# Squares moved by 4 transfers instead of 16, and scaling chains issued ahead of splits, in a hybrid decoder block

## The chip, the cores and the metric

The kernel runs on one core of one Trainium2 chip. The metric is the device time of one execution in microseconds (us). The kernel before was timed in three runs: 2091.04, 2091.20 and 2092.34 us, median 2091.2. The engines are TensorE (PE: matrix products and transposes by a product with the identity), VectorE (DVE), ScalarE (ACT), GpSimd (POOL) and SyncE (SP), which here issues the DMA transfers. Each engine runs its own list of instructions in order and waits on semaphores for the others.

## What is computed

One layer of a pre-norm decoder block for 2048 tokens of width 1024, in float32:

```
h = rmsnorm(x, norm_mix_g);  u = h @ w_in
y_conv = gate_b * conv3(gate_c * v)
y_rnn  = rg_lru(conv4(x_r)) * gelu(g)
y = concat[rmsnorm(y_conv, g_norm_conv), rmsnorm(y_rnn, g_norm_rnn)]
x = x + y @ w_out
h = rmsnorm(x, norm_mlp_g)
x = x + square(relu(h @ w_mlp_in)) @ w_mlp_out
return rmsnorm(x, final_norm_g)
```

Here the seam between `y @ w_out` and `h @ w_mlp_in` matters: x gets its last term from w_out, is squared and summed over each token's row, scaled by 1/rms and by norm_mlp_g, and has to be turned (from tokens on partitions to the 1024 features on partitions) before it can be multiplied by w_mlp_in.

## The kernel before

The 2048 tokens are four blocks of 512 (TB), worked in pairs: blocks 0 and 1, then 2 and 3. A product of float32 matrices is made of three passes of rounded parts (hi and lo: a tile `w_hi` that ACT casts and a tile `w_lo` that DVE subtracts), and large products follow a fast scheme with 7 products in place of 8. In w_out these are numbered 6, 5, 3, 7, 4 at the place in question, each for one half (512 columns) of x in one or both blocks of the pair. `product(i, ...)` goes over the four token tiles t of a block in the order 0, 2, 1, 3 (TORDER, n counts the steps): PE multiplies (`multiply`, line 2103, result `wo_x` in PSUM), DVE adds the result to x (`add`, line 2116), then the function `behind(n, t)` issues whatever is to run beside it: `in_third` behind product 3, `in_seventh` behind 7, `in_fourth` behind 4. Products 3, 7 and 4 share few PSUM buffers, so a step of one waits for an add of the product ahead.

Between w_out and the MLP the two blocks of a pair go different ways, both from a scaled tile `xs` (line 2377 on DVE, 2378 on ACT, one half each; the scale comes from `square`, line 2354 on ACT, and the chain of small instructions in `root`, lines 2365 to 2372).

- The first block (b) is turned without PE. DVE transposes 32x32 squares of `xs` into the tile `cut` (line 2391); then `move_squares` (line 2400) has the DMA queue move them to their partitions, into four tiles `raw0`, 16 transfers of 128 KB: for each of 4 token tiles a, 32 partitions of `cut` to 32 partitions of `raw0[a]`, 4 times. `gain_rows` (line 2421) multiplies by norm_mlp_g, `first_hi` (2425, ACT) and `first_lo` (2430, DVE) split the tiles into operands H.
- The second block (b + 1) is turned by PE: `turn` (line 1984) makes eight transposes of `xs` into PSUM, and ACT copies them out with the gain (line 1991).

The x of the second block's first half comes from DRAM by two loads of 512 KB (`load_x_half`, line 2122). Product 7 adds to its other half, product 4 to this one. Behind product 4 come the up products of the MLP (`ups`, line 662): `ups[s].prepare(i)` splits a weight tile (lines 197 and 198), and `drain` takes results out of PSUM (line 691 on ACT, 695 on DVE, tile `snap`). The first two turns stand between product 4's last steps, the other two between the first up products; the text writes up (s, i) for product i of column block s.

The order on each engine is the order in which the code issues the work, but for pieces wrapped in `tc.high_priority(n)`, which puts them n places ahead, and in `tc.issue_after`. The lists are the same in both pairs; the second pair's place lies 1018.44 us behind the first's.

Of the kernel before, what the change touches and what calls it, by code (L numbers as in the profile page):

```python
# [11 lines left out]
AF = mybir.ActivationFunctionType  # L12
# [3 lines left out]
P = 128  # L16
SEQ = 2048
D = 1024
# [73 lines left out]
def block_kernel(  # L92
# [213 lines left out]
    def x_half(b, t, dh):  # L306
        return xt[b, t // 2, dh][:, t % 2, :]
# [1810 lines left out]
    def load_x_half(b, dh):  # L2118
        for th in range(2):
            r = temp("x")  # L2120
            r0 = b * TB + th * 256
            nc.sync.dma_start(
                r,
                x[r0 : r0 + 256, dh * 512 : dh * 512 + 512].rearrange("(t p) d -> p t d", p=P),
            )
            xt[b, th, dh] = r
# [8 lines left out]
    def pair_before_mlp(b, ups, by_hand):  # L2135
# [10 lines left out]
        def load(n):  # L2146
            for i, g in todo[:n]:
                o.load(i, g)
            del todo[:n]
# [224 lines left out]

        def scaled(b, t, rs):
            xs[t] = temp("xs")
            V.tensor_scalar(xs[t][:, 1, :], x_half(b, t, 1), rs, None, MUL)
            nc.scalar.activation(xs[t][:, 0, :], x_half(b, t, 0), AF.Copy, scale=rs)
            keep_half(b, t)

        def in_fifth(n, t):
# [14 lines left out]
        def move_squares():  # L2396
            raw0.extend(temp("raw0", (P, KD, P)) for _ in range(4))
            for a in range(4):
                for g in range(4):
                    nc.sync.dma_start(  # L2400
                        raw0[a][32 * g : 32 * g + 32],
                        cut[0][32 * a : 32 * a + 32, g].rearrange("p k t i -> p k (t i)"),
                    )

        def in_third(n, t):
            prepare(7, of(1, 0), n)
            square(b, t, 1)
            scaled(b, t, root(b, n, t))
            cut_squares(t)
            if n == 3:  # L2410
                load(3)
                move_squares()

        product(5, Y, True, in_fifth)
        product(3, Y, False, in_third)
        ups[0].load((0,))
        load_x_half(b + 1, 0)
        hw = []

        def gain_rows(a):  # L2420
            tt(raw0[a], raw0[a], gm[:, :, None].broadcast_to([P, KD, P]), MUL)
# [10 lines left out]
        def in_seventh(n, t):  # L2432
            prepare(4, of(1, 1), n)
            square(b + 1, t, 1)
            if n > 1:
                for a in (2 * n - 4, 2 * n - 3):
                    gain_rows(a)
            if n == 3:
                hw.extend(first_operands())
                for a in range(4):  # L2440
                    first_hi(0, a)
                for a in range(4):
                    first_lo(0, a)

        product(7, X, False, in_seventh)
        for a in range(4):
            first_hi(1, a)
        ups[1].load((0,))
        r1 = []

        def in_fourth(n, t):
            square(b + 1, t, 0)
            if n == 0:
                ups[0].prepare(ORDER[0])
            if n < 2:
                first_lo(1, 2 * n)
                first_lo(1, 2 * n + 1)
            if n == 2:
                ups[0].prepare(ORDER[1])
                r1.extend(temp("r1") for _ in range(4))  # L2460
            if n > 1:
                turn(xs[TORDER[n - 2]], TORDER[n - 2], r1, gm)
            scaled(b + 1, t, root(b + 1, n, t))

        product(4, X, False, in_fourth)
        ups[1].prepare(ORDER[0])
# [34 lines left out]
    def mlp(b, ups, r0, r1, t2, rest, fifth, xs, turns_at, prepared):  # L2501
# [6 lines left out]
        for n in range(-LEAD1, len(seq)):  # L2508
            m = n + LEAD1
            if prepared <= m < len(seq):  # L2510
                ups[seq[m][0]].prepare(seq[m][1])
            m = n + SUMS1
            if 0 <= m < len(seq):
                ups[seq[m][0]].sums(seq[m][1])
# [8 lines left out]
            if s == NS - 1 and i in (3, 4):  # L2523
                with tc.issue_after(made_at["snap"]):
                    downs[0].prepare(1, i - 3)
            ups[s].drain(i, Z)
            if n == 0:
                ups[2].load((0,))
            if n in turns_at:
# [162 lines left out]
```

## Time and profile before

| | |
|---|---|
| runs | 2091.04, 2091.20, 2092.34 us |
| the profiled execution | 2091.45 us, span from first to last instruction 2089.7 us, 1.75 us around it |
| PE busy | 2074.5 us, 99% of the span |
| DVE busy | 1633.5 us, 78% |
| ACT busy | 1137.6 us, 54% |
| DMA | 226 GB/s over the span |

A row of the timeline is one instruction or several of a kind (x8), with its start, its length, and in brackets how long the engine idled before it and which instruction or transfer ended that. A transfer's row on SP is only its issue; it lands later.

### The profile page before, as it was taken

What the parts mean: (1) busy time and instruction counts of PE and PEld (TensorE: products, weight loads), DVE (VectorE), ACT (ScalarE), POOL (GpSimd) and SP (SyncE); (2) the same over time, 40 slices, a digit from 0 to 9 for tenths busy, and PEclk for the clock granted to TensorE, in tenths of its full rate; (3) what the DMA queues carried; (4) which work ended last, traced back from release to release, by engine and by line L of the source; (5) the groups of instructions that cost most, each with busy time, mean ns of one, the idle gap of its engine ahead of it and who ended that gap; (6) DMA issues with size and microseconds to landing.
All of it is one profiled execution on the core that took longest, in us unless ns stands there. A gap on an engine that the chain in (4) does not pass through costs nothing.

```text
span 2089.7 us, 24956 instructions
## 1 busy us (share of the span) xinstructions
PE 2074.5 (99%) x9262; PEld 1707.0 (82%) x9262; DVE 1633.5 (78%) x1867; ACT 1137.6 (54%) x1485; POOL 46.4 (2%) x75
## 2 busy tenths in 40 slices
PE   9999999999999999999999999999999999999998
PEld 8888788878888888888888887887788888888887
DVE  6789898579766878999987776876876665887776
ACT  6789863366655544444555887233853333533344
POOL 0011000000000000000000100000000000000000
PEclk9999999999999999999999999999999999999999
DMA  9489688763788687777384557676353445844432
GB/s 341 163 304 326 246 329 343 261 213 117 258 317 283 256 301 303 270 285 279 121 312 168 205 181 271 243 272 221 127 186 114 169 161 211 343 151 151 141 121 81
DMA packets 200330, 477.77 MB, mean 229 GB/s; under 512 B 15504, under 2 KB 80016, under 8 KB 200208
## 3 DMA queue, kind: packets, MB, share of 16 engines
q1 hardware_dynamic: 198608, 471.45, 62.5%
q10 hardware_dynamic: 1568, 4.72, 0.6%
q8 instruction: 73, 1.20, 0.2%
q14 instruction: 49, 0.40, 0.1%
q0 software_dynamic: 32, 0.00, 0.0%
HBM read 313.58 MB, written 158.33 MB: 226 GB/s over the span
## 4 chain that ended last, share of the span: by engine, by line
PE 79%; DVE 8%; ACT 5%; issue 2%; DMA 1%; SPq 0%; POOL 0%; DVEq 0%; ACTq 0%; POOLq 0%
PE up L662 39%; PE dn L785 28%; PE wo_x L2103 4%; PE wo_w L2103 3%; PE wo_y L2103 2%; DVE xr L1303 1%; ACT r L1324 1%; DVE v L1360 1%; PE ps_b L256 1%; ACT gi L1331 1%; DMA x<-in_x_dram 1%; PE psri L1771 1%; ACT r L1991 1%; DVE w_lo L1244 1%; PE ps_c L256 1%
## 5 line engine op out<-in xcount | busy, mean ns | idle before, releaser
L662 PE MATMUL up<-H,w_hi 128*128 128x512 f32 x2576 | 795.2, 390 | 1.9 <-DVE snap L695 1.9
L662 PEld LDWEIGHTS up<-H,w_hi 128*128 128x128 f32 x2576 | 482.1, 188 | 105.3 <-ACT snap L691 2.6
L662 PE MATMUL up<-H,w_lo 128*128 128x512 f32 x1288 | 501.3, 389 | 0.0
L785 PE MATMUL dn<-w_hi,z_hi 128*128 128x512 f32 x864 | 336.1, 389 | 0.0
L785 PE MATMUL dn<-w_lo,z_hi 128*128 128x512 f32 x864 | 336.1, 389 | 0.0
L785 PE MATMUL dn<-w_hi,z_lo 128*128 128x512 f32 x864 | 336.1, 389 | 0.0
L662 PEld LDWEIGHTS up<-H,w_lo 128*128 128x128 f32 x1288 | 241.7, 188 | 50.5 <-DVE w_lo L198 0.2
L197 ACT CAST z_hi<-z 128x1024 fp32r<-128x1024 f32 x112 | 118.0, 1053 | 289.4 <-PE dn L785 243.9
L198 DVE TENSOR_TENSOR w_lo<-w,w_hi 128x1024 fp32r<-128x1024 f32 x156 | 190.0, 1220 | 78.5 <-ACT w_hi L197 29.0
L197 ACT CAST w_hi<-w 128x1024 fp32r<-128x1024 f32 x156 | 163.0, 1049 | 116.3 <-PE up L662 61.5
L785 PEld LDWEIGHTS dn<-w_hi,z_lo 128*128 128x128 f32 x864 | 162.2, 188 | 33.8
L785 PEld LDWEIGHTS dn<-w_hi,z_hi 128*128 128x128 f32 x864 | 162.2, 188 | 33.7
L785 PEld LDWEIGHTS dn<-w_lo,z_hi 128*128 128x128 f32 x864 | 162.2, 188 | 33.5
L817 DVE TENSOR_TENSOR x<-dn,x 128x1024 f32<-128x1024 f32 x108 | 130.9, 1218 | 22.3 <-PE dn L785 22.1
L198 DVE TENSOR_TENSOR z_lo<-z,z_hi 128x1024 fp32r<-128x1024 f32 x112 | 136.2, 1216 | 3.1 <-ACT z_hi L197 3.1
L2103 PE MATMUL wo_x<-w_o,y_hi 128*128 128x512 f32 x384 | 118.9, 391 | 1.6 <-DVE x L2116 1.6
L2103 PEld LDWEIGHTS wo_x<-w_o,y_hi 128*128 128x128 f32 x384 | 71.6, 188 | 17.2 <-DVE x L2116 2.5
L679 ACT ACTIVATE snap<-snap 128x1024 f32<-128x1024 f32 x36 | 38.2, 1061 | 71.5 <-DVE snap L707 27.6
L2103 PE MATMUL wo_x<-w_o,y_lo 128*128 128x512 f32 x192 | 74.9, 390 | 0.0
L2103 PE MATMUL wo_w<-w_o,y_hi 128*128 128x512 f32 x192 | 59.0, 389 | 0.0
L674 ACT COPY snap<-up 128x1024 f32<-128x1024 f32 x32 | 32.4, 1014 | 39.4 <-PE up L662 34.6
L198 DVE TENSOR_TENSOR w_lo<-t,w_hi 128x1024 fp32r<-128x1024 f32 x32 | 39.0, 1218 | 18.8 <-PE dn L785 14.3
(430 smaller groups left out, 3201.9 us busy)
## 6 DMA issues: line engine op xcount, KB each, us to landing
z<-d_z SPq DMA_DIRECT2D x112, 512.0 KB, 5.6
w_o<-d_sum SPq DMA_DIRECT2D x84, 512.0 KB, 7.1
w<-in_w_mlp_in_dram SPq DMA_DIRECT2D x64, 512.0 KB, 6.7
d_z<-snap SPq DMA_DIRECT2D x64, 512.0 KB, 3.1
d_sum<-sum_hi SPq DMA_DIRECT2D x49, 512.0 KB, 4.8
d_z<-z SPq DMA_DIRECT2D x48, 512.0 KB, 3.4
w<-in_w_mlp_out_dram SPq DMA_DIRECT2D x48, 512.0 KB, 8.7
raw<-in_w_in_dram SPq DMA_DIRECT2D x30, 512.0 KB, 6.8
```

The costliest lines, as they stand in the source:

```text
L197: nc.scalar.copy(hi, src)
L198: return (lo_engine or V).tensor_tensor(lo, src, hi.bitcast(F32), SUB).ins
L256: nc.tensor.matmul(ps[:, j, :], ws[k // 4][:, k % 4, j * P : (j + 1) * P], hs(k), start=k == 0 and i == 0, stop=k == KD - 1 and i == len(p ...
L662: nc.tensor.matmul(ps[:, j, :], ws[:, k, j * P : (j + 1) * P], hs(k), start=i in (1, 2, 5) and k == 0 and n == 0, stop=k == 3 and n == len ...
L674: made_at["snap"] = nc.scalar.copy(t, ps).ins
L679: nc.scalar.activation(t, t, AF.Relu)
L785: nc.tensor.matmul(ps[t // 2][:, t % 2, :], zs[:, p, t * P : (t + 1) * P], ws[:, p, :], start=i in (1, 2, 5) and a == 0 and p == 0 and n == 0,
L817: V.tensor_add(xt[b, th, dh], ps[th], xt[b, th, dh])
L1244: tt(lo, r, hi.bitcast(F32), SUB)
L1303: stt(o, x_in[:, j, k : k + TB], par("rnn_conv_w", 8 * k + c), o, MUL, ADD)
L1324: nc.scalar.activation(r[own, j, :], ps[own, e, :], AF.Sigmoid, bias=par("b_a", c)[own])
L2103: nc.tensor.matmul(ps[t // 2][:, t % 2, :], ys[:, j, t * P : (t + 1) * P], ws[:, j, :], start=first and n == 1, stop=final and n == 6 * le ...
```

## The change

Four things change, all at this seam.

1. `move_squares` issues one transfer for each token tile in place of four: 512 KB from the same 32 partitions of `cut` to all 128 of `raw0[a]`, so that four neighbouring partitions of `raw0` come from one partition of `cut`. The features of the turned rows thereby stand in another order on the partitions (index 4q + g for 32g + q). The rows of w_mlp_in and norm_mlp_g are put in that order before the program starts (`crossed`), and block b + 1, which is turned by PE, gets the same order by writing `xs` with its columns crossed (`scaled`, for odd b).
2. The x loads of block b + 1 are issued ahead of the moves.
3. `gain_rows`, `first_operands` and `first_hi` are issued one step of product 7 earlier, all eight `first_hi` together.
4. In product 4 the chain `root` and `scaled` comes ahead of `first_lo` and of the splits of `ups[0]`, the first two turns are issued one step later, and the first splits and one drain of the MLP get a higher priority.

```diff
         def scaled(b, t, rs):
             xs[t] = temp("xs")
-            V.tensor_scalar(xs[t][:, 1, :], x_half(b, t, 1), rs, None, MUL)
-            nc.scalar.activation(xs[t][:, 0, :], x_half(b, t, 0), AF.Copy, scale=rs)
+            to = [xs[t][:, i, :] for i in range(2)]
+            of = [x_half(b, t, i) for i in range(2)]
+            if b % 2:
+                to = [a.rearrange("p (k q g) -> p k g q", k=4, g=4) for a in to]
+                of = [a.rearrange("p (k g q) -> p k g q", k=4, g=4) for a in of]
+            V.tensor_scalar(to[1], of[1], rs, None, MUL)
+            nc.scalar.activation(to[0], of[0], AF.Copy, scale=rs)
...
             for a in range(4):
-                for g in range(4):
-                    nc.sync.dma_start(
-                        raw0[a][32 * g : 32 * g + 32],
-                        cut[0][32 * a : 32 * a + 32, g].rearrange("p k t i -> p k (t i)"),
-                    )
+                nc.sync.dma_start(
+                    raw0[a].rearrange("p k t -> p (k t)"),
+                    cut[0][32 * a : 32 * a + 32].rearrange("p g k t i -> p (g k t i)"),
+                )
...
             if n == 3:
                 load(3)
+                load_x_half(b + 1, 0)
                 move_squares()
...
         ups[0].load((0,))
-        load_x_half(b + 1, 0)
...
-            if n > 1:
-                for a in (2 * n - 4, 2 * n - 3):
-                    gain_rows(a)
+            if n == 1:
+                gain_rows(0)
+                gain_rows(1)
+            if n == 2:
+                gain_rows(2)
+                gain_rows(3)
+                hw.extend(first_operands())
+                for i in range(2):
+                    for a in range(4):
+                        first_hi(i, a)
             if n == 3:
-                hw.extend(first_operands())
-                for a in range(4):
-                    first_hi(0, a)
                 for a in range(4):
                     first_lo(0, a)
...
         def in_fourth(n, t):
+            if n == 3:
+                turn(xs[TORDER[1]], TORDER[1], r1, gm)
             square(b + 1, t, 0)
-            if n == 0:
-                ups[0].prepare(ORDER[0])
+            scaled(b + 1, t, root(b + 1, n, t))
             if n < 2:
                 first_lo(1, 2 * n)
                 first_lo(1, 2 * n + 1)
+                ups[0].prepare(ORDER[n])
             if n == 2:
-                ups[0].prepare(ORDER[1])
                 r1.extend(temp("r1") for _ in range(4))
-            if n > 1:
-                turn(xs[TORDER[n - 2]], TORDER[n - 2], r1, gm)
-            scaled(b + 1, t, root(b + 1, n, t))
+                turn(xs[TORDER[0]], TORDER[0], r1, gm)
...
             if prepared <= m < len(seq):
-                ups[seq[m][0]].prepare(seq[m][1])
+                with tc.high_priority(SOONER) if m < 6 else nullcontext():
+                    ups[seq[m][0]].prepare(seq[m][1])
...
-            ups[s].drain(i, Z)
+            with tc.high_priority(SOONER) if n < 6 and i == 2 else nullcontext():
+                ups[s].drain(i, Z)
...
+    def crossed(a):
+        return _np.asarray(a).reshape(len(a), 4, P // 4, -1).swapaxes(1, 2).reshape(len(a), P, -1)
...
-        "mlp_g_t": lambda: rows("norm_mlp_g").T,
+        "mlp_g_t": lambda: crossed(rows("norm_mlp_g").T[None])[0],
+        "w_mlp_in": lambda: crossed(_np.reshape(inputs["w_mlp_in"], (KD, P, -1))).reshape(1, D, -1),
```

PE's and POOL's lists of instructions stay as they were. How the others move is shown in the first pair; the second is alike. SP's list, from the last w_o loads of product 3 (d_sum is where the weights wait in DRAM, raw_35xx are the four raw0 tiles), before:

```order
L2088 DMA w_o<-d_sum 128x1024 x2
L2400 DMA raw_3534<-cut 32x1024 x4
L2400 DMA raw_3535<-cut 32x1024 x4
L2400 DMA raw_3536<-cut 32x1024 x4
L2400 DMA raw_3537<-cut 32x1024 x4
L622 DMA w_3554<-in_w_mlp_in_dram 128x4x256
L622 DMA w_3556<-in_w_mlp_in_dram 128x4x256
L2122 DMA x<-in_x_dram 128x2x512 x2
L622 DMA w_3673<-in_w_mlp_in_dram 128x4x256
L622 DMA w_3675<-in_w_mlp_in_dram 128x4x256
```

and after the change:

```order
L2088 DMA w_o<-d_sum 128x1024 x2
L2122 DMA x<-in_x_dram 128x2x512 x2
L2404 DMA raw_3538<-cut 128x1x1024
L2404 DMA raw_3539<-cut 128x1x1024
L2404 DMA raw_3540<-cut 128x1x1024
L2404 DMA raw_3541<-cut 128x1x1024
L622 DMA w_3546<-in_w_mlp_in_dram 128x4x256
L622 DMA w_3548<-in_w_mlp_in_dram 128x4x256
L622 DMA w_3661<-in_w_mlp_in_dram 128x4x256
L622 DMA w_3663<-in_w_mlp_in_dram 128x4x256
```

The x loads now stand ahead of the moves, and the 16 moves of 32 partitions are 4 of 128.

DVE's list, from product 7's third add (the first row) to the second add of product 4 (raw_35xx times gm is `gain_rows`, H from raw is `first_lo`), in two pieces, before:

```order
L2116 SCALAR_TENSOR_TENSOR x<-wo_x,rB,x 128x512
L198 TENSOR_TENSOR y_lo<-u,y_hi 128x1024
L2421 TENSOR_TENSOR raw_3534<-raw_3534,gm 128x1024
L2421 TENSOR_TENSOR raw_3535<-raw_3535,gm 128x1024
L2116 SCALAR_TENSOR_TENSOR x<-wo_x,rB,x 128x512
L2421 TENSOR_TENSOR raw_3536<-raw_3536,gm 128x1024
L2421 TENSOR_TENSOR raw_3537<-raw_3537,gm 128x1024
L2430 TENSOR_TENSOR H_3659<-raw_3534,H_3659 128x4x128
L2430 TENSOR_TENSOR H_3659<-raw_3535,H_3659 128x4x128
L2430 TENSOR_TENSOR H_3659<-raw_3536,H_3659 128x4x128
L2430 TENSOR_TENSOR H_3659<-raw_3537,H_3659 128x4x128
L2116 SCALAR_TENSOR_TENSOR x<-wo_x,rB,x 128x512
```

```order
L198 TENSOR_TENSOR w_lo<-w_3554,w_hi 128x1024
L2430 TENSOR_TENSOR H_3660<-raw_3534,H_3660 128x4x128
L2430 TENSOR_TENSOR H_3660<-raw_3535,H_3660 128x4x128
L2365 TENSOR_SCALAR ss_3585<-ss_3585 128x4
L2368 SCALAR_TENSOR_TENSOR rs_a<-ss_3585,ss_3696 128x1
L2370 RECIPROCAL rs_s<-rs_s 128x1
L2371 SCALAR_TENSOR_TENSOR rs_q<-rs_s,rs_a 128x1
L2372 SCALAR_TENSOR_TENSOR rs_x<-rs_q,rs_s 128x1
L2377 TENSOR_SCALAR xs<-x,rs_x 128x512
L2116 SCALAR_TENSOR_TENSOR x<-wo_x,rB,x 128x512
```

and after the change, from the split behind product 7's second add:

```order
L198 TENSOR_TENSOR y_lo<-y_raw,y_hi 128x1024
L2425 TENSOR_TENSOR raw_3538<-raw_3538,gm 128x1024
L2425 TENSOR_TENSOR raw_3539<-raw_3539,gm 128x1024
L2116 SCALAR_TENSOR_TENSOR x<-wo_x,rB,x 128x512
L198 TENSOR_TENSOR y_lo<-u,y_hi 128x1024
L2425 TENSOR_TENSOR raw_3540<-raw_3540,gm 128x1024
L2425 TENSOR_TENSOR raw_3541<-raw_3541,gm 128x1024
L2116 SCALAR_TENSOR_TENSOR x<-wo_x,rB,x 128x512
L2434 TENSOR_TENSOR H_3627<-raw_3538,H_3627 128x4x128
L2434 TENSOR_TENSOR H_3627<-raw_3539,H_3627 128x4x128
L2434 TENSOR_TENSOR H_3627<-raw_3540,H_3627 128x4x128
L2434 TENSOR_TENSOR H_3627<-raw_3541,H_3627 128x4x128
```

```order
L2116 SCALAR_TENSOR_TENSOR x<-wo_x,rB,x 128x512
L2365 TENSOR_SCALAR ss_3573<-ss_3573 128x4
L2368 SCALAR_TENSOR_TENSOR rs_a<-ss_3573,ss_3684 128x1
L2370 RECIPROCAL rs_s<-rs_s 128x1
L2371 SCALAR_TENSOR_TENSOR rs_q<-rs_s,rs_a 128x1
L2372 SCALAR_TENSOR_TENSOR rs_x<-rs_q,rs_s 128x1
L2382 TENSOR_SCALAR xs<-x,rs_x 128x4x4x32
L2434 TENSOR_TENSOR H_3628<-raw_3538,H_3628 128x4x128
L2434 TENSOR_TENSOR H_3628<-raw_3539,H_3628 128x4x128
L198 TENSOR_TENSOR w_lo<-w_3546,w_hi 128x1024
L2116 SCALAR_TENSOR_TENSOR x<-wo_x,rB,x 128x512
```

The two pairs of `gain_rows` stand one add earlier, the first ahead of product 7's third add and the second ahead of its last, and between product 4's first add and xs nothing is left but the chain.

ACT's list behind product 7, from the last `first_hi` to the second scaled tile, before:

```order
L2425 CAST H_3660<-raw_3537 128x4x128
L2354 ACTIVATE rows,ss_3696<-x 128x512
L197 CAST w_hi<-w_3554 128x1024
L2369 ACTIVATE rs_s<-ss_3585,ss_3696 128x1
L2378 ACTIVATE xs<-x,rs_x 128x512
L2354 ACTIVATE rows,ss_3696<-x 128x512
L2369 ACTIVATE rs_s<-ss_3585,ss_3696 128x1
L2378 ACTIVATE xs<-x,rs_x 128x512
```

and after the change:

```order
L2429 CAST H_3628<-raw_3541 128x4x128
L2354 ACTIVATE rows,ss_3573<-x 128x512
L2354 ACTIVATE rows,ss_3684<-x 128x512
L2369 ACTIVATE rs_s<-ss_3573,ss_3684 128x1
L2383 ACTIVATE xs<-x,rs_x 128x4x4x32
L197 CAST w_hi<-w_3546 128x1024
L2354 ACTIVATE rows,ss_3684<-x 128x512
L2369 ACTIVATE rs_s<-ss_3573,ss_3684 128x1
L2383 ACTIVATE xs<-x,rs_x 128x4x4x32
```

The cast w_hi of the first up weights moved from ahead of the chain to behind xs; the copies out of the first turn (tps, not in these rows) moved behind the third xs.

## Rows read from the trace of the kernel before

**Rows 1.** The page of before, sections 1 and 2: busy times; granted clock in 40 slices.

```profile
PE 2074.5 (99%) x9262; PEld 1707.0 (82%) x9262; DVE 1633.5 (78%) x1867; ACT 1137.6 (54%) x1485; POOL 46.4 (2%) x75
...
PEclk9999999999999999999999999999999999999999
```

**Rows 2.** Waits of PE, whole span: engine, line, released by; total, times, longest.

```profile
PE tps L1984 <- ACT xs L2378: 3.4, 2, 1.8
PE up L662 <- DVE snap L695: 1.9, 2, 1.0
PE wo_x L2103 <- DVE x L2116: 1.6, 2, 1.4
```

**Rows 3.** PE over time: start us, us, engine, line, operation, out<-in [idle before <-releaser].

```profile
430.05 0.62 PE L2103 MATMUL wo_x<-w_o,y_hi 128*128 128x512 f32 x2
...
434.13 0.62 PE L2103 MATMUL wo_x<-w_o,y_hi 128*128 128x512 f32 x2
...
438.61 0.73 PE L2103 MATMUL wo_x<-w_o,y_hi 128*128 128x512 f32 x2 [0.24 <-DVE x L2116]
...
444.73 1.06 PE L1984 MATMUL tps<-ident,xs 128*128 128x128 f32 x8 [1.75 <-ACT xs L2378]
...
480.69 0.70 PE L662 MATMUL up<-H,w_hi 128*128 128x512 f32 x2 [0.90 <-DVE snap L695]
...
1458.19 0.73 PE L2103 MATMUL wo_x<-w_o,y_hi 128*128 128x512 f32 x2 [1.38 <-DVE x L2116]
```

**Rows 4.** DVE over time, same columns, product 7 to the first turn, first pair.

```profile
427.97 2.35 DVE L2421 TENSOR_TENSOR raw<-raw,gm 128x1024 f32<-128x1024 f32 x2
...
433.19 2.49 DVE L2430 TENSOR_TENSOR H<-raw,H 128x512 fp32r<-128x512 f32 x4
437.80 0.75 DVE L2116 SCALAR_TENSOR_TENSOR x<-wo_x,rB,x 128x512 f32<-128x512 f32 x1 [2.13 <-DMA x<-in_x_dram]
440.28 1.23 DVE L198 TENSOR_TENSOR w_lo<-w,w_hi 128x1024 fp32r<-128x1024 f32 x1 [1.73 <-ACT w_hi L197]
...
443.86 0.49 DVE L2377 TENSOR_SCALAR xs<-x,rs_x 128x512 f32<-128x512 f32 x1
```

**Rows 5.** SP (it issues the DMAs) over time, same columns, first pair.

```profile
416.06 1.58 SPq L2088 DMA_DIRECT2D w_o<-d_sum  x2
419.25 10.74 SPq L2400 DMA_DIRECT2D raw<-cut  x16
...
431.27 1.01 SPq L2122 DMA_DIRECT2D x<-in_x_dram  x2
```

**Rows 6.** Line 2122 (x loads), 405 to 460 us.

```profile
DMA to landing us min/median/max: 6.4/6.8/7.2
```

**Rows 7.** Line 2400 (moves of squares), 405 to 460 us.

```profile
L2400 SPq DMA_DIRECT2D raw<-cut x16: 508/588/601, 419.2 to 429.4; - x16
...
DMA to landing us min/median/max: 2.3/2.5/5.4
```

**Rows 8.** DMA view, 385 to 450 us, 40 slices of 1.6 us; busy times, 470 to 480.

```profile
GB/s 333 300 403 113 5 0 93 366 280 366 416 393 23 0 0 0 71 252 416 403 265 396 310 217 194 224 199 212 158 364 330 324 389 379 79 0 0 10 0 302
...
470.00:480.00 10.00, 9.79 (x44) 7.77 (x42) 10.00 (x14) 6.91 (x16) 0.00 (x0) 1.00 0.01 2
```

**Rows 9.** ACT over time, columns as in rows 3, first pair.

```profile
431.78 4.27 ACT L2425 CAST H<-raw 128x512 fp32r<-128x512 f32 x8
...
439.22 1.03 ACT L197 CAST w_hi<-w 128x1024 fp32r<-128x1024 f32 x1
...
443.86 0.72 ACT L2378 ACTIVATE xs<-x,rs_x 128x512 f32<-128x512 f32 x1 [0.68 <-DVE rs_x L2372]
...
454.42 2.15 ACT L1991 ACTIVATE r<-tps,gm 128x128 f32<-128x128 f32 x8
```

**Rows 10.** Line 2088 (w_o loads), first pair, 416 to 417 us.

```profile
DMA to landing us min/median/max: 4.9/6.4/7.8
```

**Rows 11.** Line 2088, second pair, 1430 to 1437 us.

```profile
DMA to landing us min/median/max: 5.9/7.1/8.3
```

More of the change, by code (lines that the diff above doesn't have):

```diff
@@ L2445, in pair_before_mlp @@
         product(7, X, False, in_seventh)
-        for a in range(4):
-            first_hi(1, a)
         ups[1].load((0,))
```

## The prediction

> **What bounds the kernel now.** [...] The list of PE's waits comes next [rows 2]: six waits inside the program, 3.4 us for the scaled squares xs, 1.9 us for snap, 1.6 us for an add of w_out's result, 6.9 us in all. Each costs a little more than its idle time: steps of product 4 are 4.08 us apart (430.05 to 434.13), the next starts 4.48 us later with 0.24 us of idle, the turn at 444.73 is 2.04 us late with 1.75 us [rows 3]. With some 0.2 us of that kind each the six come to about 8.2 us, 0.4% of the time: 3.6 in the first pair of blocks (0, 1), 4.6 in the second. That is all this change can win, and 0.2% (4.2 us) is about what a measurement can tell from no change.
>
> Why PE waits there is read back along the queues. In VectorE's (DVE's) rows the add of product 4 at 437.80 idles 2.13 us for a DMA, the x of the next block [rows 4]. SyncE (SP) issued that load at 431.27, behind 16 moves of squares that took it 10.74 us to issue [rows 5], and it landed 6.4 and 7.2 us later [rows 6]. After the add come w_lo, which waits for ScalarE (ACT), and two first_lo; only then the chain of small instructions to xs at 443.86 [rows 4], and PE's turn begins when ACT's half of xs is done.
>
> **What the change removes.** The x loads go ahead of the moves. SP stood waiting between w_o's second issue (done 417.64) and the moves at 419.25, so their 1.01 us of issuing [rows 5] hide there, and x is in place by about 425: the 2.13 us go. w_lo and first_lo go behind the chain. xs of the first step would be ready 1.8 us (square, root, 0.72 us of scaling) after the add, over 2 us before PE asks. All six waits of [rows 2] then go, except what comes back below. The 24 fewer DMA issues free SP some 8 us per pair, and nobody waits for SP after that: worth nothing. The w_mlp_in rows and the gain are reordered on the host: nothing, the loads keep sizes and count. PE's own instructions are unchanged, and so is GpSimd's list.
>
> **What it adds: a wait on the moves.** In DVE's new order two gain_rows, which need moves 0 and 1, stand ahead of product 7's third add, and two, which need moves 2 and 3, ahead of its last add. PE's product 4 waits for the first of these adds before its step 0 (it takes over the PSUM it reads), and for the other before its next step. Before, the first pair stood ahead of the last add only and the second pair behind it. So the landing of the moves now sets when PE starts product 4.
>
> When do they land? The last of the old moves was issued at 429.4 and landed 2.3 to 2.5 us later, 431.8 [rows 7]. The queue's slices of 1.6 us from 422.4 to 432 carry 158 to 224 GB/s, while the loads beside them carry 400 to 416 [rows 8]. The first of the old moves came out of a backlog (up to 5.4 us after issue [rows 7]), so SP's issuing was not the limit there: the moves themselves are slow. 2.1 MB between 422.3 and 431.8 are 222 GB/s, or 2.36 us for each new transfer of 512 KB; a load takes 1.3 us. The new transfers still read 32 partitions each, but write all 128. I take the old rate. [...]
>
> Two w_o loads start when d_x has landed (419.8) and end at 422.4, x at 425.0 by the load rate, then the moves at 427.3, 429.65, 432.0 and 434.4. Step 0 of product 4: gain 1 starts at 429.65, the add 1.2 us later and lasts 0.75 [rows 4], so PE starts at 431.6 in place of 430.05: **+1.57**. Next step, due at 435.7: gain 3 from 434.4, add done 436.3: **+0.64**. In the second pair PE's place runs 1018.44 us later, and w_o took 1 us longer to land there (5.9 against 4.9 for the first of the two [rows 10, 11]): moves 1 and 3 land at 1449.1 and 1453.8, PE is due at 1448.5: **+2.58** and **+0.64**. Sum +5.4, against 8.2 removed: **−2.8**, if everything else is free.
>
> **What is not free.** (a) xs of the odd blocks is now written in steps of 16 bytes, 4 times per pair on DVE and on ACT. No row of before has such a write. From below it costs nothing; from above, DVE goes from 0.49 us to somewhat over the 0.62 of first_lo, which reads two inputs of this size (4 in 2.49 [rows 4]), so 0.3 more at most, and ACT adds at most 0.4 us to 0.72 (at twice the elements, w_hi's cast of 1024, a row takes 1.03 us [rows 9]). I take 0.2 on both, DVE's pair of rows being the nearest. Walking the new order row by row with the durations of the rows, that leaves PE waiting 0.2 to 0.3 us for product 4's add before up (0,1) and 0.5 for ACT's copies of the turned squares (8 in 2.15 [rows 9]) before up (1,1), so 0.75 us per pair: **+1.5**; at the upper bound +3.3. [...] (b) w_o's second load landed as late as 7.8 us after its issue [rows 10], 424.4, not 422.4, beside the moves. If the loads ahead of the moves are later by 1 us, the moves are, and PE with them, 1 us per pair: 0 to +2, for 1 us, +4 for 2. I take half a microsecond: **+1**. (c) The 8 first_hi on ACT (4.27 us [rows 9]) start at 434.4 instead of 431.8 and end at 438.7, before the next add to be squared (439.6): nothing; if that cover is gone they push the chain.
>
> Sum: −8.2 + 5.4 + 1.5 + 1.0 = −0.3; by the walk, which lets small slacks absorb some of it, −0.5. Bounds of this case: −3.0 (a and b free) to about +3 (0.3 and 0.4 us on xs, 1 us on w_o). The profiled execution took 2091.45 us, 0.25 over the median of the runs, 2091.2, so I set the change on the median: **2090.7 us**.
>
> **Rivals.**
> 1. *The moves run at the load rate*, 1.3 us each, since all 128 partitions are written and few large transfers are made. For it: the later of the old moves landed as SP issued them, 2.3 to 2.5 us after their issue each and one in 0.6 us, so part of the old rate may be SP's. Against: the slices of 422 to 427, with the backlog, are no faster than the others [rows 8]. They land from 426.2 to 430.1, the new waits shrink to nothing in the first pair and 0.5 us in the second, and 7 to 8 us are won, 5 with xs dear, 3 with w_o late: 2083.5 to 2088, say 2085.
> 2. *Slower: DVE's queue holds the adds behind late moves.* The place is gain_rows ahead of product 7's adds. The break-even is a move of about 2.8 us; from 3.3 us each the change is slower by over 0.2%. It decides if the new spread makes more DMA engines read the same part of SBUF at once: a source partition of 16 KB now goes to four neighbouring destinations, where the old moves paired 32 with 32. At half the old rate (4.7 us) move 1 lands at 434.4 and move 3 at 443.8, PE waits 6.3 + 5.3 us in the first pair and 7.3 + 5.3 in the second, 24 in all, less the 8.2: +16, 2107. Against it: the bytes read per partition are the same as before.
> 3. *What is won comes back at the next full engine.* DVE is busy for all of 470 to 480 [rows 8], and up (2,2) already waits 0.90 us for its snap [rows 3]. If PE arrives sooner there, it waits there longer; DVE's sum of work is unchanged. Then even with quick moves 0 to −2: 2090. It also covers that the loads collide and x still comes late.
>
> **How the numbers follow.** Forecast 0.50, rival 1 0.22, rival 2 0.16, rival 3 0.12. Faster by over 4.2 us: 0.19 of rival 1, and 0.07 from the forecast and rival 3 where the moves are a quarter quicker (1.85 us each: −1 to −6): 0.26. Slower: 0.15 of rival 2 and 0.06 of the forecast beyond its bounds (w_o 2 us late with xs dear, or moves of 3 us): 0.21. The rest, 0.53, is no change. The range takes in rival 1 down to 2084.5 and rival 2 where moves are slowed by up to half (3.5 us, +5 to +6): 2097. The forecast's own range is 2088 to 2094.
>
> **What would show it.** Right: no DVE idle for x, no PE wait for xs at the turns, x issued before the moves; a PE wait at wo_x of 1.5 and 2.6 us ended by DVE's add of product 7, whose queue waits on the moves' landing; moves 2.3 to 2.5 us apart. Rival 1 shows moves 1.3 us apart and no wait there; rival 2 the same wait several times as long; rival 3 waits at up (1,1) and (2,2) of over 1 us. The size of (a) stands in the durations of xs. If PE waits somewhere that I have not named, or DVE's or ACT's rows of other shapes grew, the argument is wrong and not only its sizes.

## The result and the profile after

The changed kernel takes 2096.01 us (median of 13 runs; one, at 2987 us with a granted clock of 0.65, is left out of the ratio), the kernel before 2091.2 (13 runs): a ratio of 1.0023 with a 95% interval of 1.0014 to 1.0031, so 2.9 to 6.5 us slower. The profiled execution has a span of 2093.6 us against 2089.7, 3.9 us more, and shows where these come from; the other 0.9 us of the difference between the medians stand in no profile. First all waits of PE (columns as in [rows 2]):

```profile
PE wo_x L2103 <- issue: 3.9, 2, 2.4
PE up L662 <- ACT r L1991: 1.5, 2, 0.8
PE start_x L447 <- POOL ones_raw L272: 1.1, 1, 1.1
PE wo_x L2103 <- DVE x L2116: 1.0, 1, 1.0
PE up L662 <- DVE x L2116: 0.7, 2, 0.4
PE up L662 <- DVE w_lo L198: 0.5, 1, 0.5
```

The waits of [rows 2] for xs and for snap are gone, and so is that of [rows 3] at 438.61. In their place stand 4.9 us ahead of product 4 (the "issue" rows are its first steps; no releaser is found for them, and DVE's list below names it), 0.7 and 1.5 us ahead of two up products, and 0.5 us much later. On PE over time:

```profile
432.01 0.70 PE L2103 MATMUL wo_x<-w_o,y_hi 128*128 128x512 f32 x2 [1.54 <-issue]
...
437.40 0.73 PE L2103 MATMUL wo_x<-w_o,y_hi 128*128 128x512 f32 x2 [1.03 <-DVE x L2116]
...
452.01 0.73 PE L662 MATMUL up<-H,w_hi 128*128 128x512 f32 x2 [0.28 <-DVE x L2116]
...
465.72 0.72 PE L662 MATMUL up<-H,w_hi 128*128 128x512 f32 x2 [0.76 <-ACT r L1991]
...
1453.40 0.90 PE L2103 MATMUL wo_x<-w_o,y_hi 128*128 128x512 f32 x2 [2.36 <-issue]
```

The wait for w_lo stands alone, some 80 us behind the seam:

```profile
565.08 0.50 PE L662 MATMUL up<-H,w_lo 128*128 128x512 f32 x1 [0.53 <-DVE w_lo L198]
```

DVE over time in the first pair, to be held against [rows 4]: its queue stands still for the moves, and product 7's third add comes directly behind.

```profile
428.48 1.23 DVE L2425 TENSOR_TENSOR raw<-raw,gm 128x1024 f32<-128x1024 f32 x1 [4.25 <-DMA raw<-cut]
430.02 1.23 DVE L2425 TENSOR_TENSOR raw<-raw,gm 128x1024 f32<-128x1024 f32 x1 [0.31 <-DMA raw<-cut]
431.16 0.74 DVE L2116 SCALAR_TENSOR_TENSOR x<-wo_x,rB,x 128x512 f32<-128x512 f32 x1
...
434.20 2.48 DVE L2425 TENSOR_TENSOR raw<-raw,gm 128x1024 f32<-128x1024 f32 x2 [1.16 <-DMA raw<-cut]
436.60 0.74 DVE L2116 SCALAR_TENSOR_TENSOR x<-wo_x,rB,x 128x512 f32<-128x512 f32 x1
...
442.18 0.70 DVE L2382 TENSOR_SCALAR xs<-x,rs_x 128x512 f32<-128x512 f32 x1
```

The add's end at 431.9 is the start of PE's product 4 (432.01), and the add at 436.60 that of its next step (437.40). ACT's half of the first strided xs, which took 0.72 us in [rows 9]:

```profile
442.18 1.23 ACT L2383 ACTIVATE xs<-x,rs_x 128x512 f32<-128x512 f32 x1 [0.68 <-DVE rs_x L2372]
```

SP over time, against [rows 5]: the moves take 3.00 us to issue instead of 10.74, and the four loads behind them 10.50 us instead of 2.15, while the moves ahead of them have not landed (they land at 428.4, 430.0, 434.2 and 435.4). SP is done with these loads at 433.6, as before (433.4).

```profile
417.57 1.17 SPq L2122 DMA_DIRECT2D x<-in_x_dram  x2
419.51 3.00 SPq L2404 DMA_DIRECT2D raw<-cut  x4
423.08 10.50 SPq L622 DMA_DIRECT2D w<-in_w_mlp_in_dram  x4
```

What the DMA queue carried from 385 to 450 us, in slices as in [rows 8]:

```profile
GB/s 295 315 418 164 0 0 78 300 345 323 401 411 78 0 0 0 58 207 416 406 232 267 339 219 333 417 348 267 240 292 340 338 291 139 29 5 10 0 0 0
```

And one thing of which the prediction has nothing. Busy times by stretch in the second pair (length; PE, PEld, DVE, ACT, POOL busy; granted clock; DMA share; GB/s), around and behind the wait of 2.36 us:

```profile
1452.00:1453.40 1.40, 0.00 (x0) 0.03 (x1) 1.40 (x3) 0.01 (x1) 0.00 (x0) 1.00 1.04 231
1453.40:1455.00 1.60, 1.60 (x5) 1.27 (x6) 1.03 (x1) 0.72 (x2) 0.00 (x0) 0.61 0.86 245
1455.00:1457.00 2.00, 2.00 (x6) 1.60 (x5) 1.23 (x1) 0.00 (x0) 0.00 (x0) 0.50 0.88 258
1457.00:1459.00 2.00, 2.00 (x10) 1.54 (x8) 1.50 (x2) 1.50 (x3) 0.00 (x0) 0.96 1.03 349
```

After PE had stood for 2.36 us the granted clock fell from 1.00 to 0.50 for some 3.5 us; matmuls then start 0.43 us apart instead of 0.23.

Since PE's list is the same in both kernels, each matmul can be held against its own start in the other profile. That difference is constant for long stretches and steps where PE waits. The steps, each from one constant stretch to the next (us, after less before):

| | first pair | second pair | both |
|---|---|---|---|
| waits ahead of product 4, for adds behind the moves | +1.8, +1.4 | +2.5, +0.4 | +6.1 |
| PE at the lower clock behind the longest of them | none | +1.7 | +1.7 |
| up (0,1) and up (1,1) | +0.6, +1.0 | +0.7, +1.0 | +3.3 |
| a wait for w_lo at 565.08 | +1.0 | none | +1.0 |
| waits of before that went (add, turn, snap) | −0.5, −2.0, −1.1 | −1.7, −1.9, −1.2 | −8.4 |
| start of the program | | | +0.3 |

The sum is +4.0, and the last matmul starts 4.0 us later.

### The profile page after: what moved, and what is told of

Same layout as the page of the kernel before. It is cut to its first block, busy times and chain, and to the rows that moved or that the text cites. A ratio compares the mean times of both kernels' runs of the same rounds, so it can differ in the third digit from the quotient of the medians.

```text
span 2093.6 us, 24930 instructions
## 1 busy us (share of the span) xinstructions
PE 2077.5 (99%) x9262; PEld 1708.8 (82%) x9262; DVE 1634.9 (78%) x1867; ACT 1140.1 (54%) x1485; POOL 45.9 (2%) x75
## 4 chain that ended last, share of the span: by engine, by line
PE 78%; DVE 7%; ACT 6%; DMA 3%; issue 2%; SPq 0%; POOL 0%; ACTq 0%; DVEq 0%; POOLq 0%
PE up L662 39%; PE dn L785 28%; PE wo_x L2103 3%; PE wo_w L2103 3%; PE wo_y L2103 2%; DMA raw<-cut 1%; DVE xr L1303 1%; DVE v L1360 1%; PE ps_b L256 1%; PE psri L1771 1%; DVE w_lo L1244 1%; ACT r L1324 1%; ACT r L1991 1%; PE ps_c L256 1%; PE ps_v L256 1%
```

## The experiments

The theory: adds of product 7 and 4 stand in DVE's list behind work that waits for the moves; the moves, not SP, are slow (in the first pair the four land within 8.4 us behind x and are issued in 3.00), and four large ones land no sooner; the strided xs costs PE another 3 us. The rivals are named with each run. Every run was compared with the kernel before on its own chip; ratios are to that.

**Only part 3 taken back** (gain_rows, first_operands, first_hi where they stood).

```diff
-            if n == 1:
-                gain_rows(0)
-                gain_rows(1)
-            if n == 2:
-                gain_rows(2)
-                gain_rows(3)
-                hw.extend(first_operands())
-                for i in range(2):
-                    for a in range(4):
-                        first_hi(i, a)
+            if n > 1:
+                for a in (2 * n - 4, 2 * n - 3):
+                    gain_rows(a)
             if n == 3:
+                hw.extend(first_operands())
+                for a in range(4):
+                    first_hi(0, a)
...
         product(7, X, False, in_seventh)
+        for a in range(4):
+            first_hi(1, a)
```

> The changed kernel with only part 3 taken back: gain_rows, first_operands and first_hi stand where they stood before. Theory (the adds of product 7 are held behind the landing of the moves, and the long stall lets TensorE's clock fall in the second pair): no wait ahead of product 4's first step, the granted clock stays at its upper level there, a wait of up to 1.7 us is left at product 4's third step (first_lo still stands ahead of the add and waits for the last move); 2090 to 2092.5 us, 3.5 to 6 us less than the changed kernel. Rival (the strided writes of xs and the later loads make the loss, the wait on the moves is hidden anyway): 2094.5 to 2097.

Measured 2093.25 us, 1.0007 (0.9998 to 1.0016): by the ratios 3.3 of the 4.8 us go, and the time lies between the two forecasts. The waits ahead of product 4's first two steps are gone. But the stop has only moved one add on, as DVE's rows show:

```profile
435.90 2.57 DVE L2425 TENSOR_TENSOR raw<-raw,gm 128x1024 f32<-128x1024 f32 x2 [3.50 <-DMA raw<-cut]
438.38 2.49 DVE L2434 TENSOR_TENSOR H<-raw,H 128x512 fp32r<-128x512 f32 x4
440.80 0.74 DVE L2116 SCALAR_TENSOR_TENSOR x<-wo_x,rB,x 128x512 f32<-128x512 f32 x1
```

PE waits 2.38 us there in the first pair and 2.26 in the second. Only with the second of these does the clock fall (first pair, then second):

```profile
441.60:443.50 1.90, 1.90 (x8) 1.59 (x9) 0.91 (x6) 1.19 (x4) 0.00 (x0) 1.00 0.08 28
...
1461.90:1463.60 1.70, 1.68 (x4) 1.40 (x5) 0.74 (x5) 1.01 (x3) 0.00 (x0) 0.50 0.10 35
```

I had allowed 1.7 us; the last move landed at 437.2, not 435.4 as in the changed kernel.

**xs written straight.** The odd blocks' features then meet the wrong rows of w_mlp_in.

```diff
-            if b % 2:
+            if b % 2 > 1:
```

> The changed kernel with xs of the odd blocks written straight, not in steps of 16 bytes (the features of the odd blocks then meet the wrong rows of w_mlp_in). Theory: the scaling rows go back to 0.49 us on DVE and 0.72 us on ACT, the waits ahead of up (0,1) (0.3 and 0.4 us) and up (1,1) (0.8 and 0.7 us) go, 2 to 3.1 us less than the changed kernel: 2092.5 to 2094. Rival (the chain has slack, those waits come from the order of ACT's copies of the turned squares): 2095 to 2097, the waits stay.

Measured 2093.36 us, 1.0008 (0.9999 to 1.0017), some 3 us less than the changed kernel by the ratios. The waits of PE in the MLP's first products are gone; only those for the moves are left (the "issue" row is again the first step of product 4):

```profile
PE wo_x L2103 <- DVE x L2116: 3.6, 2, 1.9
PE wo_x L2103 <- issue: 3.4, 2, 1.7
...
PE up L662 <- DVE w_lo L198: 0.3, 1, 0.3
```

So +3.3 in the table is the price of the strided writes: both steps at up (0,1) and up (1,1) are gone here. It comes by the chain to up (0,1) and by ACT's copies out of the turns, which stand behind the longer xs rows. That the total falls by as much is partly chance: the fall of the clock went too (1.7 us), and the waits for the moves grew from 6.1 to 8.2 us, as the last move of the first pair landed at 436.6 in place of 435.4.

**Part 1 taken back: 16 moves, straight xs.** In `scaled`, in the table of inputs and here the lines of before are put back:

```diff
             for a in range(4):
-                nc.sync.dma_start(
-                    raw0[a].rearrange("p k t -> p (k t)"),
-                    cut[0][32 * a : 32 * a + 32].rearrange("p g k t i -> p (g k t i)"),
-                )
+                for g in range(4):
+                    nc.sync.dma_start(
+                        raw0[a][32 * g : 32 * g + 32],
+                        cut[0][32 * a : 32 * a + 32, g].rearrange("p k t i -> p k (t i)"),
+                    )
```

> The changed kernel with only part 1 taken back: 16 moves of 128 KB, straight xs, weights in their own order; x still ahead of the moves, gain_rows still ahead of the adds. Theory: the moves run at their old rate of 210 to 220 GB/s, so move group 1 lands 1 to 2 us later than the 430.0 of the changed kernel; the wait ahead of product 4 is longer by that (both pairs), the strided cost of 3 us is gone; 2093 to 2097. Rival (the four large moves are themselves the loss, because they read one quarter of the partitions into all): waits shorter than in the changed kernel, 2088 to 2091.

Measured 2094.6 us, 1.0010 (1.0001 to 1.0019). The theory holds: the waits are longer (3.74 and 2.98 us), and the clock falls with them in both pairs: to 0.50 from 434.4 to 436.0 in the first, and in the second matmuls start 0.43 us apart.

```profile
PE wo_x L2103 <- issue: 6.7, 2, 3.7
```

The data of moves 0 and 1, for which product 4's first step waits, had all landed at 432.2 in this run and at 430.0 in the changed kernel, and PE started that step at 434.37 and at 432.01. The last one landed at 436.8 here and at 435.4 in the changed kernel; over all runs with x ahead it is 435.7 to 436.8 with 16 and 435.4 to 437.2 with four. So four large moves bring the first data some 2 us sooner and the last no sooner.

**Parts 1 and 3 taken back: x ahead of 16 moves, chains ahead of splits.** The edits of the first and of the last run together.

> The changed kernel with parts 1 and 3 taken back: what is left is x ahead of the moves and the chains ahead of splits. Theory: no wait ahead of product 4, no strided cost, the wait for x gone, a wait of 1.5 to 2.5 us left at product 4's third step because first_lo ahead of its add waits for the last move, snap's wait of 1 us gone: 2088 to 2091. Rival (what is won comes back at the up products, since VectorE is full there): 2091 to 2092, with new waits at up (1,1) and up (2,2).

Measured 2089.51 us, 0.9991 (0.9982 to 1.0000). PE's waits are what the theory says: nothing but the adds of product 4 (4.9 us in 3 waits, the longest 2.4). The theory leaves out the clock, which falls behind the longest of them, in the first pair:

```profile
443.00:445.00 2.00, 2.00 (x7) 1.52 (x6) 2.00 (x4) 1.49 (x2) 0.00 (x0) 0.50 0.03 8
```

**Part 1 alone, on the kernel before.** The moves, `scaled` and the table of inputs are those of the changed kernel.

> The kernel before with part 1 alone: four large moves, the strided xs, the rows of w_mlp_in in the new order; x stays behind the moves, all orders as before. Theory (the DMA queue is limited by its bytes there, not by SP's issuing): SP is done issuing 8 us sooner, yet x lands at 436 to 439 as before, the waits of before stay, and the strided writes add 1 to 2 us per pair: 2092.5 to 2096. Rival (SP's 10.7 us of issuing kept x late): x lands by 433, the waits for x and for xs go: 2087 to 2090.

Measured 2096.32 us, 1.0021 (1.0012 to 1.0030): 0.3 us beyond the slow end of the theory. The profiled execution is the fastest of the eleven (2094.65 us); in it the waits of before stay and grow, 9.2 us in place of 6.9, without a fall of the clock (its mean over the execution is 1.0). What the other executions lose beyond that stands in no profile. SP issues x at 432.70, later than the 431.27 of [rows 5], although it has 12 fewer transfers to issue per pair:

```profile
420.04 7.60 SPq L2404 DMA_DIRECT2D raw<-cut  x4
427.73 4.92 SPq L622 DMA_DIRECT2D w<-in_w_mlp_in_dram  x2
432.70 1.01 SPq L2122 DMA_DIRECT2D x<-in_x_dram  x2
```

The issuing of four moves takes 7.60 us here. The last of them was issued by 427.7 and landed at 433.9, where the last of the 16 was issued at 429.4 and landed at 431.8; x landed at 439.2 and 440.5, 1.5 us later than before. This takes the ground from my first rival: SP's issuing was not what held the moves.

**Part 2 alone: only the x loads moved ahead.**

```diff
                 load(3)
+                load_x_half(b + 1, 0)
                 move_squares()
...
         ups[0].load((0,))
-        load_x_half(b + 1, 0)
```

> The kernel before with part 2 alone: the two x loads ahead of the 16 moves. Theory: x lands by 429, but the last move lands at 436 to 437 in place of 431.8, and product 4's first add stands behind gain_rows and first_lo, which wait for it: it runs at about 440 in place of 437.8, PE waits 2 us or more there, the clock falls after it, the wait ahead of the turn stays: 2093 to 2097. Rival (x was what came last): both waits go, 2086 to 2089.

Measured 2093.84 us, 1.0009 (1.0000 to 1.0018). x is there early, and the add still stands behind the last move, gain_rows and first_lo (DVE, first pair):

```profile
436.58 1.23 DVE L2421 TENSOR_TENSOR raw<-raw,gm 128x1024 f32<-128x1024 f32 x1 [0.79 <-DMA raw<-cut]
437.72 2.49 DVE L2430 TENSOR_TENSOR H<-raw,H 128x512 fp32r<-128x512 f32 x4
440.13 0.74 DVE L2116 SCALAR_TENSOR_TENSOR x<-wo_x,rB,x 128x512 f32<-128x512 f32 x1
```

The add ran at 437.80 in [rows 4]. The clock falls to 0.50 in both pairs of the profiled execution, behind waits of 1.84 and 2.39 us, as expected. What I had not expected: the waits ahead of the turns are gone, since PE now comes 2 us and a slower stretch later to them. The run with parts 1 and 3 taken back is this one with part 4 added: 0.9991 against 1.0009, so by the ratios part 4 brings some 3.8 us on top of part 2.

**A new order: nothing that needs the last moves ahead of product 4's first add and chain.** 16 moves, straight xs; on top of the run with parts 1 and 3 taken back:

```diff
-            if n > 1:
-                for a in (2 * n - 4, 2 * n - 3):
-                    gain_rows(a)
             if n == 3:
-                hw.extend(first_operands())
-                for a in range(4):
-                    first_hi(0, a)
-                for a in range(4):
-                    first_lo(0, a)
+                gain_rows(0)
+                gain_rows(1)
...
-        for a in range(4):
-            first_hi(1, a)
...
             scaled(b + 1, t, root(b + 1, n, t))
-            if n < 2:
-                first_lo(1, 2 * n)
-                first_lo(1, 2 * n + 1)
-                ups[0].prepare(ORDER[n])
+            if n == 0:
+                gain_rows(2)
+                gain_rows(3)
+                hw.extend(first_operands())
+                for a in range(4):
+                    first_hi(0, a)
+            if n == 1:
+                for a in range(4):
+                    first_lo(0, a)
+                for a in range(4):
+                    first_hi(1, a)
+                ups[0].prepare(ORDER[0])
             if n == 2:
                 r1.extend(temp("r1") for _ in range(4))
                 turn(xs[TORDER[0]], TORDER[0], r1, gm)
+            if n > 1:
+                first_lo(1, 2 * n - 4)
+                first_lo(1, 2 * n - 3)
+            if n == 2:
+                ups[0].prepare(ORDER[1])
```

> A new order: x ahead of 16 moves, straight xs, and in VectorE's and ScalarE's lists nothing that waits for the last two moves stands ahead of product 4's first add and its chain (gain_rows 0 and 1 behind product 7's last add, 2 and 3 behind the first xs, first_hi and first_lo behind that). Theory: no wait at product 4 and none at the first turn, all 7 to 8 us of the old waits are won: 2083 to 2086. Rival (VectorE is full up to 505 us, what is won comes back ahead of the up products): waits of 1 us or more at up (0,1), (1,1) or (2,2), 2087 to 2091.

Measured 2097.37 us, 1.0023 (1.0014 to 1.0032): a miss. Product 4 and the turns wait for nothing any more, but first_lo of the second operand now comes behind the last xs, and up (0,2) needs it:

```profile
PE up L662 <- DVE H L2430: 7.0, 2, 3.5
...
PE up L662 <- ACT r L1991: 1.3, 2, 0.6
```

Two waits of 3.48 us, and with both the clock goes down (here the first; behind the second, matmuls start 0.43 us apart):

```profile
460.10:462.00 1.90, 1.83 (x4) 1.49 (x5) 1.90 (x5) 1.56 (x6) 0.00 (x0) 0.50 1.02 351
462.00:464.00 2.00, 2.00 (x6) 1.57 (x5) 1.65 (x5) 0.57 (x1) 0.00 (x0) 0.50 1.09 382
```

**The same with four moves and strided xs** (part 1 of the change put back in).

> The same new order with the four large moves and the strided xs of the change. Theory: the last move lands within 1 us of where it does with 16 moves, the strided writes lengthen each chain by 0.5 us on ScalarE: 1 to 4 us more than with 16 moves and straight xs: 2085 to 2089. Rival (with the order mended the strided writes are hidden and SP's shorter issuing pays): the same as with 16 moves or less, 2081 to 2085.

Measured 2099.59 us, 1.0032 (1.0019 to 1.0045), with the same two waits (7.2 us, the longest 3.6), and ahead of up (0,2) 2.4 us for product 4's last add in place of the 1.3 for ACT's copies. It is 2.2 us more than with 16 moves, as the theory has it, but both runs lie far above the forecast times.

**first_lo of the second operand one step sooner** (16 moves).

```diff
                 for a in range(4):
                     first_hi(1, a)
+                first_lo(1, 0)
+                first_lo(1, 1)
                 ups[0].prepare(ORDER[0])
             if n == 2:
                 r1.extend(temp("r1") for _ in range(4))
                 turn(xs[TORDER[0]], TORDER[0], r1, gm)
-            if n > 1:
-                first_lo(1, 2 * n - 4)
-                first_lo(1, 2 * n - 3)
-            if n == 2:
+                first_lo(1, 2)
+                first_lo(1, 3)
                 ups[0].prepare(ORDER[1])
```

> The order of the run with chains first and 16 moves, with first_lo of the second operand (the low parts that up (0,2) waited 3.5 us for, in both pairs) one step of product 4 sooner. Theory (that one late piece, and the clock that fell behind its wait, is the whole of its 5 us loss): no wait at product 4, at the turns or for H, upper clock level throughout, only 0.6 us per pair ahead of up (0,2) for ScalarE's copies out of the turns: 2085 to 2088. Rival (VectorE is full there, pulling one piece ahead pushes another behind): another wait of 1.5 us or more at an up product, 2090 to 2095.

Measured 2085.83 us, 0.9972 (0.9961 to 0.9982). The theory holds; what is left is a wait of 0.8 us per pair for ACT's copies.

**ACT's copies out of the first turn sooner.**

```diff
+            if n == 2:
+                r1.extend(temp("r1") for _ in range(4))
+                turn(xs[TORDER[0]], TORDER[0], r1, gm)
...
             square(b + 1, t, 0)
             scaled(b + 1, t, root(b + 1, n, t))
...
             if n == 2:
-                r1.extend(temp("r1") for _ in range(4))
-                turn(xs[TORDER[0]], TORDER[0], r1, gm)
                 first_lo(1, 2)
```

> As the run before, with ScalarE's copies out of the first turn ahead of the squares of product 4's third step, in the 1.95 us that ScalarE idles there. Theory: the last 0.6 us per pair ahead of up (0,2) go as well: 0.5 to 1.5 us less than the run before, 2083.5 to 2087. Rival (the copies delay the third xs and its turn): the same or up to 1 us more than the run before.

Measured 2083.79 us, 0.9963 (0.9951 to 0.9976): 7.6 us less than the kernel before beside it. No wait of PE at the seam is left, and the steps of PE's starts against the kernel before are the six waits that went, −8.4 us, and 0.3 at the start of the program. These are all waits that the profile has:

```profile
PE start_x L447 <- POOL ones_raw L272: 1.1, 1, 1.1
PE start_x L491 <- ACT h_hi L469: 0.2, 1, 0.2
PE ps_b L256 <- DVE w_lo L1244: 0.2, 1, 0.2
```

**That order with part 1 of the change, and that order with x behind the moves.** The first puts the lines of part 1 in again, the second moves `load_x_half` behind `move_squares`. There the two x loads stand behind the moves, but ahead of the two w loads, which they followed in the kernel before.

> The order of the last run (chains first, low parts and turn copies sooner) with part 1 of the change: four large moves and strided xs. Theory (the strided writes cost 0.5 us on ScalarE and 0.2 us on VectorE each, on the chain that leads to up (0,1); the four moves land no sooner than the 16): waits of about 1 us per pair ahead of up (0,1), 1 to 4 us more than with 16 moves: 2085 to 2088. Rival (with the order mended there is slack for the strided writes): 2083 to 2084.5.

> The order of the run with turn copies sooner and 16 moves, but x loaded behind the moves as in the kernel before: part 2 taken back. Theory: the waits for product 4's first add are back (0.4 and 1.6 us in the kernel before, for x that lands at 438), the waits at the turns and for snap stay away because the order mends them: 2085 to 2087. Rival (x ahead is what the whole gain hangs on): the waits at the turns are back too, 2089 to 2091.

Measured 2084.63 us, 0.9962 (0.9948 to 0.9976), and 2084.3 us, 0.9960 (0.9948 to 0.9973). Beside the last run neither can be told apart by its ratio. So with the chains first there is slack for most of the strided writes: PE loses 0.5 us at up (0,1) in each pair, with waits of 0.2 us for ACT's copies, and the time lies between the forecast and its rival. (With x behind the moves, where xs is straight, the same 0.5 us stand in the second pair, so not all of it is the price of the writes.) And x need not be ahead of the moves: behind them, and ahead of the w loads, it landed at 434.8 and 436.1, in time for the add. Both that run's forecast and its rival were too slow: no wait came back at product 4.

## Why the prediction was wrong

It said 2090.7 us, no change, and gave 0.21 to slower; the result is 4.8 us slower than before. The range (2084.5 to 2097) holds it, the direction does not. Two steps failed: term (a), the strided writes, taken at +1.5 us and measured at +3.3, and the price of a new wait, taken at its length and 0.2 us, where the longest one also brought 1.7 us at the lower clock. A wait outside the seam, which the sum does not have, added 1.0 us.

- **What goes: right.** −8.2 in the sum, −8.4 measured, with each of the six waits gone. The last orders show that all of it can be had.
- **The wait on the moves: mechanism right, size near, in part by luck.** PE's start of product 4 was forecast at 431.6 and came at 432.0, the next step's at 436.3 and came at 437.4, with the two adds as releasers. Sum +5.4 with +1.0 for a late w_o; measured +6.1. Two errors inside nearly cancel in the first pair: w_o landed at 424.3, the late case of (b), and x 2 us later than my 425.0, but the first two moves landed after 1.3 and 1.6 us in place of 2.36. The next two landed after 4.2 and 1.3 us, so the sign of 2.3 to 2.5 us between moves did not appear. In the second pair move 1 landed 2.3 us later than forecast, and so was PE, which by then had lost 2.4. The four took 8.4 us behind x in the first pair and 10.3 in the second, 2.1 and 2.6 us each on average: about the old rate, which I had taken over from [rows 7, 8]. 2.1 MB in 8.4 to 10.3 us are 203 to 250 GB/s, where loads carry over 400 [rows 8]. What sets this rate was not shown: the slice of 1.6 us from 427.3, right behind x, carried 348 GB/s, with none of the w loads among the moves yet, and from 431 on these ran beside them.
- **The strided xs: mis-sized, step (a).** I took +0.2 us on both engines and at most +0.4 on ACT. DVE took 0.70 instead of 0.49 (+0.21), ACT 1.23 instead of 0.72 (+0.51). The bound came from a row that writes straight, so it bounded nothing. PE lost 3.3 us to it in place of 1.5, at the two places named; that is what the prediction has for its upper bound. Why the strided write is slower, and costs ACT more than DVE, was not shown.
- **The clock: missing from the sum.** I priced a wait at its length and some 0.2 us. Behind the 2.36 us in the second pair PE ran for 3.5 us at a granted clock down to 0.50, 1.7 us more. My step treated a new wait as worth as much as an old one, yet the waits that went (1.75 us the longest) had cost no clock (1.00 from 442 to 446 and from 1462 to 1466), and the one that came did.
- **+1.0 at 565 us: not foreseen.** A w_hi cast on ACT (562.74) is late behind a load of x's next rows, for which ACT waits 2.66 us, in the kernel before 1.00. It shows up in some runs (0.8 us with xs straight, 1.1 with 16 moves, 0.3 with part 3 taken back) and not in others. No run was made for it, and its cause stays open. By the prediction's own last sentence a wait at a place not named counts against the argument, and not only its sizes.
- **SP's saved issuing: right that it is worth nothing**, but not for the reason given. It is not saved: the next loads' issues grew from 2.15 to 10.50 us.

By terms: −0.3 forecast; strided xs +1.8, clock +1.7, the wait at 565 +1.0, the removed waits −0.2 and the moves −0.3 make 3.7, and 0.3 at the start of the program the 4.0 of the table. Rival 2's place was therefore right, and it decided without its condition: on average the moves were not slower than before. Each was merely in front of the adds, and the long wait was dearer than its length. Rival 3 (what is won comes back at a full engine) falls: in the last orders nothing comes back, though DVE is busy for all 26 us from 464 to 490 there.

## What to carry to other kernels

In a list that runs in order, ask of every instruction what it waits for and who stands behind it: work that needs a slow transfer belongs behind the adds that free PSUM for the engine that sets the pace. Reorder until that engine's list of waits is empty, one late piece at a time; here this gained 7.6 us with the old transfers, and the new transfers added nothing to it. Don't count fewer issues as a gain while the transfers ahead have not landed and the next issues are held (here 10.50 us for four loads in place of 2.15), and price a wait of the pacing engine from its length only up to the longest that the trace shows without a fall of the clock (1.75 us in the kernel before).

## What was not expected of the hardware

- A strided write of 128x512 float32 in steps of 16 bytes takes ACT 1.23 us instead of 0.72, DVE 0.70 instead of 0.49.
- PE's idle time and its granted clock, in the profiled executions. Behind waits of 2.98 us and more the clock fell each time, to 0.50 where the stretch was read (3.74 and 2.98 us with 16 moves, 3.48 twice in the first new order); in the same order with four moves, with 7.2 us in two waits, the mean clock over the execution is 0.996, against 0.997 in the first new order and 0.999 in the next. Behind the seam's waits of 1.75 us and less it never fell. Between, length alone doesn't say. It fell behind 1.84 and 2.39 us with x ahead alone, 2.36 in the changed kernel, 2.26 with part 3 taken back and 2.44 with parts 1 and 3 taken back. It did not fall behind 2.38 and 2.29 in the other pairs of these last two runs, behind two waits of 4.4 us together with part 1 alone (mean clock 1.0), or behind 1.92 with xs straight. What else decides was not tried. By the granted clock of the stretches a fall costs 1.5 to 2.4 us more (1.5 with 16 moves, 1.7 in the changed kernel, 2.4 in the first new order). In some runs the fall comes 1.3 to 1.5 us after PE is back at work (parts 1 and 3 taken back, x ahead alone), in others it comes while PE still waits (with 16 moves, first pair, where the clock is 0.97 on average from 430 to 434.3).
- The issuing of four loads took 10.50 us while transfers ahead had not landed, where it took 2.15 us before. What holds it was not tried.
